# Storing the gated attention output as scaled fp16 halves and loading it through transposing DMAs

## The chip, the cores and the metric

One Trainium2 chip, one of its cores. The metric is the device time of one launch in microseconds (us). A change of under 0.2% (2.9 us here) is treated as no change.

## The reference

An encoder block for 2048 tokens of width 1024. Only the last steps bear on this change:

```python
proj = rms_norm(x, norm_w) @ w_in                     # split into u_f, g_f, q, k, v, g_a
y_f = Fourier(u_f) * silu(g_f)                        # 512 wide
# q, k, v: 3 dilation configurations x 8 slots of 64; outs and lses of each
alpha = softmax(stack(lses), axis=0)
o = sum(alpha[..., None] * stack(outs), axis=0)       # (2048, 512)
y_a = o * silu(g_a)
y = x + concatenate([y_f, y_a], axis=-1) @ w_out      # mixed is 1024 wide
```

## The kernel before

Matrix products are kept near fp32 accuracy by splitting an operand into a high and a low part and adding three products (high x high, high x low, low x high). The input projection does this with fp16 parts and weights scaled by powers of two, the output projection with parts of the type fp32r.

The work is a list of items, each one accumulation on TensorE into a PSUM tile `psq` (three buffers). Twelve units of q, k and v come first (`inproj`, L307), with the attention of earlier units beside them. Four tail units U to U+3 follow: `chan` items (L569) give gate and input of the Fourier half by channel, and `tok` items (L585), called tok 0 to tok 15 below, give the attention gate g_a for 256 tokens each, tok 0 to 7 in unit U+2 and tok 8 to 15 in unit U+3. Between tok 7 and tok 8 stand the four `chan` items of unit U+3. While one unit multiplies, `w_prep` prepares the weights `wh` of the next, in eight chunks k: ScalarE (ACT) writes the high part (L284), VectorE (DVE) the low part (L286). One step of the item loop emits everything that belongs beside the item, so every engine's order is fixed by the text of the loop in `body`; nothing is reordered afterwards.

Beside the tok items, `og_all` combines the three attention outputs: SyncE (SP) loads a tile `ot` of 256 tokens from DRAM (four buffers), POOL copies its statistics out, DVE multiplies (L696) and adds (L701, L703) into a tile `yo` (eight buffers). When tok q is through on TensorE, `ga_out` makes silu of the gate: ACT reads `psq` twice (L594, L595) into a tile `ye` (two buffers), DVE finishes silu (L596) and multiplies it into `yo` (L712). `ya_st` then stores `yo` to the DRAM tensor `YA` from SP's queue, which holds the `ot` loads and the loads `dr` of the DFT matrix (L745) as well.

After the last item comes `tail_`. SP loads `Y`, the Fourier gate, 4 MB (L853), into the room that the transposed input held, and the rows `wor` of w_out behind it (L857). The DFT runs in four parts: `f_trans` (L769, evacuated by L771 on ACT and L772 on DVE into `at`) and `f_dft` (L802, L807, evacuated by L811, L818, L819 and multiplied into `Y`). `wo_prep` splits w_out beside them (L867, L868).

The last stage is 16 rows of 128 tokens. For a row, `o_in` loads the 128 tokens of `YA` and of x, `o_mix_a` transposes `YA` on TensorE (four 128x128 transposes, L894, PSUM tile `pya`) and splits it into the tile `mx` (L895 on ACT, L896 on DVE), `o_mix_y` does the split for the Fourier half (L901, L903), and `o_mm` runs 48 matmuls of 512 columns (L917), the four attention blocks of K first. `o_in(r + 2)` stands ahead of `o_mm(r)`, and `o_mix_a(r + 1)` at its head, so in row 0 its transposes stand after the first 24 matmuls and in the others before the first.

Of the kernel before, what the change touches and what calls it, by code (L numbers as in the profile page):

```python
# [11 lines left out]
F32 = mybir.dt.float32  # L12
F32R = mybir.dt.float32r
F16 = mybir.dt.float16
BF16 = mybir.dt.bfloat16
I32 = mybir.dt.int32
AF = mybir.ActivationFunctionType
OP = mybir.AluOpType
AX = mybir.AxisListType
# [3 lines left out]
S, D = 2048, 1024  # L23
# [67 lines left out]
class Kernel:  # L91
# [615 lines left out]
    def ga_out(self, u, q):  # L707
        ps = self.PS.pop((u, q))
        y = self.YO[q].rearrange("p r w -> p (r w)")
        e = self.gp.tile([128, 2, 512], F32, name="ye", tag="ye", bufs=2)  # L710
        self.silu(e[:, 0], ps, self.W[u][1], e[:, 0], e[:, 1])
        self.nc.vector.tensor_tensor(y, y, e[:, 0], OP.mult)  # L712
        self.YD.append(q)

    def ya_st(self, q):
        hf, g = divmod(q, 8)
        dst = self.YA[g * 256:g * 256 + 256, hf * 256:hf * 256 + 256].rearrange("(r p) w -> p r w", p=128)
        self.nc.sync.dma_start(dst, self.YO.pop(q))

    def fourier_consts(self):  # L720
        nc, a = self.nc, self.a
# [137 lines left out]
    def wo_prep(self, nh, wo):  # L859
        nc = self.nc  # L860
        V, A = nc.vector, nc.scalar
        for k in range(KT):
            n = nh * KT + k + 2
            if n < 2 * KT:
                self.wo_load(*divmod(n, KT))
            raw = self.WR.pop((nh, k))
            A.copy(wo[k][:, 0], raw)  # L867
            V.tensor_tensor(wo[k][:, 1], raw, wo[k][:, 0].bitcast(F32), OP.subtract)  # L868
            yield

    def o_in0(self):
        ya = self.dp.tile([128, 2, 512], F32, name="ya0", tag="dr", bufs=2)[:, 0]
        self.nc.sync.dma_start(ya, self.YA[0:128])
        m = self.ap.tile([128, 2, 4, 512], F32R, name="mx0", tag="at", bufs=2)
        self.OI[0], self.MX[0] = ya, m[:, 0].rearrange("p a n -> p (a n)").rearrange("p (a k n) -> p a k n", a=2, k=KT)

    def o_in(self, r):
        nc = self.nc
        if r:
            self.OI[r] = ya = self.yp.tile([128, 512], F32, name="ya", tag="ya", bufs=3)  # L880
            nc.sync.dma_start(ya, self.YA[r * 128:r * 128 + 128])
        xt = self.yp.tile([128, D], F32, name="xo", tag="xo", bufs=3)
        nc.sync.dma_start(xt, self.a["x"][0, r * 128:r * 128 + 128])
        self.XO[r] = xt

    def o_mix_a(self, r):
        nc = self.nc
        V, A = nc.vector, nc.scalar
        if r:
            self.MX[r] = self.yp.tile([128, 2, KT, 128], F32R, name="mx", tag="mx", bufs=2)  # L890
        ya, m = self.OI.pop(r), self.MX[r]
        ps = (self.pso, self.psp)[r % 2].tile([128, 4, 128], F32, name="pya", tag="op"[r % 2])
        for k in range(4):
            nc.tensor.transpose(ps[:, k], ya[:, k * 128:k * 128 + 128], self.idf)  # L894
        A.copy(m[:, 0, 4:8], ps)  # L895
        V.tensor_tensor(m[:, 1, 4:8], ps, m[:, 0, 4:8].bitcast(F32), OP.subtract)  # L896

    def o_mix_y(self, r):
        m = self.MX[r]
# [28 lines left out]
    def body(self):  # L928
        tc, nc = self.tc, self.nc
        U = self.U = len(self.units)  # L930
        tail = self.tail
        with ExitStack() as ctx:
            def pool(name, bufs=1, side="left", **k):
                return tc.alloc_tile_pool(name=name, bufs=bufs, side=side, reuse_waits="tile", **k)
            psum = [pool(n, b, space=PSUM) for n, b in (("psq", 3), ("pss", 2), ("psm", 1), ("psp", 1), ("pso", 1))]
            self.psq, self.pss, self.psm, self.psp, self.pso = psum
            drm = pool("drm", space=DRAM)
# [4 lines left out]
            ctx.enter_context(tc.manual_schedule())  # L942
            self.O = [drm.tile([S, 3, 2, UW], F32, name=f"O{i}") for i in range(2)]
            self.SG = drm.tile([4, 128, S], F32, name="SG")
            self.YA = drm.tile([S, 512], F32, name="YA")
            self.KD = drm.tile([24, HD + 3], F32, name="KD")
            for d in "W WL WS PS RAW QS QR HL TR ST QW VT BT SB PB PH OB OT DT AT OI MX OW XS XR XH XP YO WR XO".split():
                setattr(self, d, {})
            self.WQ, self.OS = [], []
            self.xT = xp.tile([128, 2, KT, S], F16, name="xT")  # L950
# [47 lines left out]
            if tail:  # L998
# [8 lines left out]
                for q in range(NT):  # L1007
                    u = U + 2 + q // 8
# [20 lines left out]
            for i in range(max(len(items) + 1, G + 32)):  # L1029
                ip, wchunks = iter(()), 0  # L1030
                if i < len(items):
                    u, _, _, gen, out = items[i]
                    ip = gen()
                    p = i - first[u]
# [150 lines left out]
                    for _ in fc:  # L1185
                        pass
            if tail:
                for q in sorted(self.YO):
                    self.ya_st(q)
                self.tail_(pool, xp, fpool)  # L1190
            else:
                for c, sp in self.units:
                    nc.sync.dma_start(self.a[f"O{c}{sp}"], self.O[sp // 2][:, c, sp % 2, :])
                for p in reversed(apools):
                    p.release()
                for p in (self.wp, self.wraw, xp):
                    p.release()
# [67 lines left out]
```

## Time and profile before

| what | value |
|---|---|
| median of 3 runs | 1427.89 us (1427.65 to 1429.28) |
| the profiled execution | 1427.95 us, span 1426.2 us |
| TensorE (PE) busy | 1390.3 us, 97% of the span |
| VectorE (DVE) busy | 986.7 us, 69% |
| ScalarE (ACT) busy | 739.4 us, 52% |
| output projection, L917 | 768 matmuls, 181.3 us busy |
| transposes of YA, L894 | 64, 9.6 us busy |
| mean granted TensorE clock | 0.994 |

The profiled execution lies 0.06 us over the median, so its rows can be used as they stand. 1.75 us of it lie outside the span. Times in the rows are counted from the start of the span. A row of the timeline gives the start, the duration, the engine, the line and, in brackets, how long the engine had been idle before and what released it; a row of the chain of waits gives the start, the duration and the line that the end of the program hung on at that time.

### The profile page before, as it was taken

The numbers are of one execution on the slowest core, as the hardware profiler recorded it, in microseconds if no ns is written. First come the engines' busy times: TensorE is split into PE (matmuls) and PEld (weight loads), VectorE is DVE, ScalarE is ACT, GpSimd is POOL, SyncE is SP. The second block draws the span as 40 slices with busy tenths as digits, with TensorE's granted clock in tenths as the row PEclk, the third lists the DMA queues.
The fourth block names the chain that finished last, engine by engine and source line by source line (L and its number), as shares of the span: only waits on it lengthen the run. The fifth ranks groups of instructions, "written<-read, shape, count | busy, mean of one in ns | idle before, by whom it ended". The sixth has DMA issues, their size and how long they took to land.

```text
span 1426.2 us, 27743 instructions
## 1 busy us (share of the span) xinstructions
PE 1390.3 (97%) x9554; PEld 1027.6 (72%) x9554; DVE 986.7 (69%) x3130; ACT 739.4 (52%) x2079; POOL 458.6 (32%) x637
## 2 busy tenths in 40 slices
PE   4999999999999999999999999999999998999998
PEld 2666666667777777778888888744448697788887
DVE  6798888887878888888877777744488776611111
ACT  6676767676766666666756666554213134300110
POOL 0254444444444444444443333320000002211110
PEclk9999999999999999999999999999999999999999
DMA  7777777676766768687846465654434237333332
GB/s 212 201 142 128 143 127 142 130 140 133 136 140 121 150 117 158 119 158 115 150 101 136 99 135 97 137 110 129 147 120 136 89 102 264 103 112 111 111 117 76
DMA packets 409485, 188.66 MB, mean 132 GB/s; under 512 B 304832, under 2 KB 391040, under 8 KB 408832
## 3 DMA queue, kind: packets, MB, share of 16 engines
q1 hardware_dynamic: 380740, 173.89, 54.5%
q10 hardware_dynamic: 28604, 13.00, 3.9%
q8 instruction: 75, 1.23, 0.4%
q14 instruction: 66, 0.54, 0.1%
HBM read 72.37 MB, written 29.76 MB: 72 GB/s over the span
## 4 chain that ended last, share of the span: by engine, by line
PE 83%; DVE 6%; DMA 5%; ACT 2%; issue 2%; POOL 1%; SPq 1%; ACTq 0%; POOLq 0%; DVEq 0%
PE psq L307 44%; PE py L917 12%; PE psq L569 12%; PE psq L585 6%; PE pS L456 3%; PE po L522 2%; DMA wor<-in_w_out_dram 2%; PE po L523 1%; DMA xs<-in_x_dram 1%; PE pS L444 1%; DVE xhl L218 1%; DMA pt<-ph 1%; DMA qw<-qw 1%; DVE wh L286 1%; ACT xjk L187 0%
## 5 line engine op out<-in xcount | busy, mean ns | idle before, releaser
L307 PE MATMUL psq<-wh,xT 128*128 128x384 f16 x4608 | 789.5, 327 | 8.2 <-ACT wh L284 4.2
L307 PEld LDWEIGHTS <-xT 128*128 128x128 f16 x4608 | 541.0, 119 | 200.1 <-issue 7.1
L492 ACT ACTIVATE P<-pS,ob,kb 128x256 f32<-128x256 f32 (+1 forms) x384 | 199.4, 526 | 150.2 <-DVE ob L484 149.8
L504 POOL TENSOR_TENSOR ph<-P,ph 128x512 f16<-128x512 f32 x160 | 189.1, 1182 | 193.8 <-ACT ph L499 171.5
L360 POOL TENSOR_TENSOR qn<-qn,kb 128x128 f32<-128x128 f32 x192 | 87.5, 456 | 295.5 <-DVE qn L359 195.9
L917 PE MATMUL py<-wo,mx 128*128 128x512 f32 x768 | 181.3, 395 | 0.4 <-DVE mx L896 0.4
L569 PE MATMUL psq<-xT,wh 128*128 128x512 f16 x768 | 168.9, 379 | 0.0
L474 DVE CUSTOM_DVE_ANT_0 pS<-pS,bt 128x256 f32<-128x256 f32 (+1 forms) x384 | 147.8, 385 | 28.2 <-PE pS L444 19.8
L917 PEld LDWEIGHTS py<-wo,mx 128*128 128x128 f32 x768 | 143.2, 188 | 32.3 <-DVE mx L896 0.8
L371 POOL TENSOR_TENSOR hl<-qn,hl 128x256 f16<-128x256 f32 x192 | 130.7, 681 | 30.2 <-ACT hl L366 30.2
L569 PEld LDWEIGHTS <-wh 128*128 128x128 f16 x768 | 74.2, 98 | 87.0 <-issue 0.8
L920 DVE TENSOR_TENSOR xo<-xo,py 128x512 f32<-128x512 f32 x32 | 22.0, 688 | 139.1 <-PE py L917 139.1
L533 DVE TENSOR_REDUCE ob<-po 128x128 f32<-128x256 f32 (+1 forms) x160 | 75.3, 470 | 55.4 <-PE po L523 55.4
L499 ACT CAST ph<-P 128x512 f16<-128x512 f32 x160 | 99.0, 619 | 8.7 <-DMA wr<-in_w_in_dram 1.3
L366 ACT CAST hl<-qn 128x256 f16<-128x256 f32 x192 | 77.1, 402 | 47.6 <-POOL qn L360 37.0
L327 DVE TENSOR_TENSOR vt<-psq,vt 128x128 f16<-128x128 f32 x192 | 55.0, 286 | 62.2 <-ACT vt L326 62.0
L326 ACT CAST vt<-psq 128x128 f16<-128x128 f32 x192 | 51.2, 267 | 82.5 <-PE po L523 82.5
L286 DVE SCALAR_TENSOR_TENSOR wh<-wr,nws,wh 128x384 f16<-128x384 f32 x128 | 86.6, 682 | 2.6 <-ACT wh L284 2.6
L895 ACT CAST mx<-pya 128x512 fp32r<-128x512 f32 x16 | 9.4, 587 | 148.0 <-issue 124.9
L585 PE MATMUL psq<-wh,xT 128*128 128x256 f16 x768 | 84.3, 273 | 0.0
L585 PEld LDWEIGHTS <-xT 128*128 128x128 f16 x768 | 75.2, 98 | 9.1
L318 ACT COPY raw<-psq 128x256 f32<-128x256 f32 x192 | 69.3, 361 | 21.1 <-PE psq L307 20.6
(158 smaller groups left out, 1774.9 us busy)
## 6 DMA issues: line engine op xcount, KB each, us to landing
wr<-in_w_in_dram SPq DMA_DIRECT2D x104, 192.0 KB, 2.8
ot<-O SPq DMA_DIRECT2D x16, 792.0 KB, 4.6
st<-st SPq DMA_DIRECT2D x96, 128.0 KB, 2.6
xs<-in_x_dram SPq DMA_DIRECT2D x16, 512.0 KB, 5.3
xo<-in_x_dram SPq DMA_DIRECT2D x16, 512.0 KB, 3.5
out_dram<-xo SPq DMA_DIRECT2D x15, 512.0 KB, 2.9
O<-ob ACTq DMA_DIRECT2D x108, 66.0 KB, 2.6
O<-ob ACTq DMA_DIRECT2D x32, 132.0 KB, 2.4
```

Of the source, the lines that this page charges most:

```text
L286: V.scalar_tensor_tensor(wh[:, 1, k - 1, :n], wr[k - 1], nws[:, k - 1:k], wh[:, 0, k - 1, :n], op0=OP.mult, op1=OP.subtract)
L307: nc.tensor.matmul(ps[:, :384], self.xtile(j, k, c, t), wh[:, l, k, :384], start=n == 0, stop=n == 23)
L360: G.tensor_tensor(qn[:, 2:4], qn[:, 2:4], self.kf[:, h0:h0 + 2], OP.mult)
L366: self.nc.scalar.copy(hl.rearrange("p a h l d -> p (a h) l d")[:, :, 0], qn)
L371: self.nc.gpsimd.tensor_tensor(hv[:, :, 1], qn, hv[:, :, 0], OP.subtract)
L474: V.tensor_tensor_reduce(out=sS[:, h, cs], in0=ps[:, h, cs], in1=bs, scale=1.0, scalar=-3.0e38, op0=OP.add, op1=OP.max, accum_out=mx[:, e, ...
L492: self.nc.scalar.activation(P[:, h, cs], sS[:, h, cs], AF.Exp, bias=ob[:, e, 130 + h:131 + h], scale=self.om[:, h0 + h:h0 + h + 1], accum_ ...
L499: self.nc.scalar.copy(ph[:, 0], P)
L504: self.nc.gpsimd.tensor_tensor(ph[:, 1], P, ph[:, 0], OP.subtract)
L569: nc.tensor.matmul(ps, wh[:, l, k, col * 128:col * 128 + 128], self.xT[:, j, k, ch * 512:ch * 512 + 512], start=n == 0, stop=n == 23)
L585: nc.tensor.matmul(ps[:, j * 256:j * 256 + 256], self.xT[:, i, k, r * 128:r * 128 + 128], wh[:, l, k, 128:384], start=n % 24 == 0, stop=n ...
L917: nc.tensor.matmul(ps[nh], m[:, j, k], wo[nh][k][:, l], start=(j, l, k) == (0, 0, 4), stop=(j, k) == (1, 3))
```

## The change

`ga_out` scales y by a power of two and splits it into two fp16 halves: ACT writes the high half (new L718), DVE the low half (new L719), both into the second half of the tile `ye`. The scale comes from a bound on y over the column half, computed by four small DVE instructions ahead of tok 0 and tok 8 (`ya_scale`, new L727 to L730). `ya_st` stores the two halves from `ye` with two DMAs (new L737), so a buffer of `ye` is free only when both have landed. `o_in` loads each half with a transposing DMA (new L899, L908), and `o_mix_a` only converts to fp32r: one copy on ACT (new L919), one on DVE (new L920). The inverse of the scale goes into the rows of w_out that belong to the attention half (new L891, L892 beside L887, L888).

```diff
     def ga_out(self, u, q):
...
-        self.nc.vector.tensor_tensor(y, y, e[:, 0], OP.mult)
+        V = self.nc.vector
+        V.tensor_tensor(y, y, e[:, 0], OP.mult)
+        if q % 8 == 0:
+            self.ya_scale(q // 8, self.W[u][1])
+        sc = self.YS[q // 8][:, 0:1]
+        h = e[:, 1].bitcast(F16).rearrange("p (l n) -> p l n", l=2)
+        self.nc.scalar.activation(h[:, 0], y, AF.Copy, scale=sc)
+        V.scalar_tensor_tensor(h[:, 1], y, sc, h[:, 0], op0=OP.mult, op1=OP.subtract)
+        self.YO.pop(q)
+        self.YH[q] = h
         self.YD.append(q)
+
+    def ya_scale(self, hf, sb):
+        V = self.nc.vector
+        t = self.YS[hf] = self.sm.tile([128, 2], F32, name="ysc", bufs=2)
+        V.tensor_reduce(t[:, 1:2], self.IS[:, hf].rearrange("p c s h -> p (c s h)"), AX.X, OP.max)
+        V.scalar_tensor_tensor(t[:, 1:2], t[:, 1:2], 2.0 ** 16, sb[:, 1:2], op0=OP.mult, op1=OP.mult)
+        V.tensor_scalar(t[:, 0:1].bitcast(I32), t[:, 1:2].bitcast(I32), 0x7F800000, None, op0=OP.bitwise_xor)
+        V.tensor_scalar(t[:, 1:2], t[:, 1:2], 0.5, None, op0=OP.mult)
 
     def ya_st(self, q):
         hf, g = divmod(q, 8)
-        dst = self.YA[g * 256:g * 256 + 256, hf * 256:hf * 256 + 256].rearrange("(r p) w -> p r w", p=128)
-        self.nc.sync.dma_start(dst, self.YO.pop(q))
+        h = self.YH.pop(q)
+        for l in range(2):
+            dst = self.YA[l, g * 256:g * 256 + 256, hf * 256:hf * 256 + 256].rearrange("(r p) w -> p r w", p=128)
+            self.nc.sync.dma_start(dst, h[:, l].rearrange("p (r w) -> p r w", r=2))
...
     wo_prep:
-            A.copy(wo[k][:, 0], raw)
-            V.tensor_tensor(wo[k][:, 1], raw, wo[k][:, 0].bitcast(F32), OP.subtract)
+            if k < 4:
...
+            else:
+                sc = self.YS[k // 2 - 2][:, 1:2]
+                A.activation(wo[k][:, 0], raw, AF.Copy, scale=sc)
+                V.scalar_tensor_tensor(wo[k][:, 1], raw, sc, wo[k][:, 0].bitcast(F32), op0=OP.mult, op1=OP.subtract)
...
     o_in (o_in0 alike, into ya0):
-            self.OI[r] = ya = self.yp.tile([128, 512], F32, name="ya", tag="ya", bufs=3)
-            nc.sync.dma_start(ya, self.YA[r * 128:r * 128 + 128])
+            self.OI[r] = ya = self.yp.tile([128, 2, 4, 128], F16, name="ya", tag="ya", bufs=3)
+            for l in range(2):
+                nc.sync.dma_start(ya[:, l], self.YA[l, r * 128:r * 128 + 128], transpose=True)
...
     o_mix_a:
-        ps = (self.pso, self.psp)[r % 2].tile([128, 4, 128], F32, name="pya", tag="op"[r % 2])
-        for k in range(4):
-            nc.tensor.transpose(ps[:, k], ya[:, k * 128:k * 128 + 128], self.idf)
-        A.copy(m[:, 0, 4:8], ps)
-        V.tensor_tensor(m[:, 1, 4:8], ps, m[:, 0, 4:8].bitcast(F32), OP.subtract)
+        A.copy(m[:, 0, 4:8], ya[:, 0])
+        V.tensor_copy(m[:, 1, 4:8], ya[:, 1])
```

The order of the instructions on VectorE, from tok 5 to the last weight chunk of unit U+3 (the last L286). Before:

```order
L596 SCALAR_TENSOR_TENSOR ye<-ye 128x512
L712 TENSOR_TENSOR yo<-yo,ye 128x512
L670 TENSOR_TENSOR cr<-cs 128x16
L672 TENSOR_TENSOR cw<-cw,IS 128x48
L674 TENSOR_TENSOR cr<-cr,cs 128x16
L286 SCALAR_TENSOR_TENSOR wh<-wr,nws,wh 128x384
L676 RECIPROCAL cr<-cr 128x16
L678 TENSOR_TENSOR cw<-cw,cr 128x48
L596 SCALAR_TENSOR_TENSOR ye<-ye 128x512
L712 TENSOR_TENSOR yo<-yo,ye 128x512
```

After, at the same place:

```order
L596 SCALAR_TENSOR_TENSOR ye<-ye 128x512
L713 TENSOR_TENSOR yo<-yo,ye 128x512
L719 SCALAR_TENSOR_TENSOR ye<-yo,ysc,ye 128x512
L670 TENSOR_TENSOR cr<-cs 128x16
L672 TENSOR_TENSOR cw<-cw,IS 128x48
L674 TENSOR_TENSOR cr<-cr,cs 128x16
L286 SCALAR_TENSOR_TENSOR wh<-wr,nws,wh 128x384
L676 RECIPROCAL cr<-cr 128x16
L678 TENSOR_TENSOR cw<-cw,cr 128x48
L596 SCALAR_TENSOR_TENSOR ye<-ye 128x512
```

L719 stands right behind the product that it reads (L713), with nothing between them while ACT computes L718, and ahead of the weight chunks.

SP's queue in the same stage (loads `ot`, stores `YA`), as one piece of the difference:

```order
-L718 DMA YA<-yo 128x2x256 x3
+L737 DMA YA<-ye 128x2x256 x6
 L645 DMA ot<-O_102 128x2x792 x2
-L718 DMA YA<-yo 128x2x256 x4
+L737 DMA YA<-ye 128x2x256 x8
 L645 DMA ot<-O_102 128x2x792 x2
-L718 DMA YA<-yo 128x2x256
+L737 DMA YA<-ye 128x2x256 x2
```

The stores keep their places: those of tok 3 stand behind two `ot` loads, as before, but now a buffer of `ye` hangs on them.

More of the change, by code (lines that the diff above doesn't have):

```diff
@@ L866, in wo_prep @@
             raw = self.WR.pop((nh, k))
-            A.copy(wo[k][:, 0], raw)
-            V.tensor_tensor(wo[k][:, 1], raw, wo[k][:, 0].bitcast(F32), OP.subtract)
+            if k < 4:
+                A.copy(wo[k][:, 0], raw)
+                V.tensor_tensor(wo[k][:, 1], raw, wo[k][:, 0].bitcast(F32), OP.subtract)
+            else:
+                sc = self.YS[k // 2 - 2][:, 1:2]
+                A.activation(wo[k][:, 0], raw, AF.Copy, scale=sc)
+                V.scalar_tensor_tensor(wo[k][:, 1], raw, sc, wo[k][:, 0].bitcast(F32), op0=OP.mult, op1=OP.subtract)
             yield
@@ L872, in o_in0 @@
         ya = self.dp.tile([128, 2, 512], F32, name="ya0", tag="dr", bufs=2)[:, 0]
-        self.nc.sync.dma_start(ya, self.YA[0:128])
+        ya = ya.bitcast(F16).rearrange("p (l k n) -> p l k n", l=2, k=4)
+        for l in range(2):
+            self.nc.sync.dma_start(ya[:, l], self.YA[l, 0:128], transpose=True)
         m = self.ap.tile([128, 2, 4, 512], F32R, name="mx0", tag="at", bufs=2)
@@ L879, in o_in @@
         if r:
-            self.OI[r] = ya = self.yp.tile([128, 512], F32, name="ya", tag="ya", bufs=3)
-            nc.sync.dma_start(ya, self.YA[r * 128:r * 128 + 128])
+            self.OI[r] = ya = self.yp.tile([128, 2, 4, 128], F16, name="ya", tag="ya", bufs=3)
+            for l in range(2):
+                nc.sync.dma_start(ya[:, l], self.YA[l, r * 128:r * 128 + 128], transpose=True)
         xt = self.yp.tile([128, D], F32, name="xo", tag="xo", bufs=3)
@@ L944, in body @@
             self.SG = drm.tile([4, 128, S], F32, name="SG")
-            self.YA = drm.tile([S, 512], F32, name="YA")
+            self.YA = drm.tile([2, S, 512], F16, name="YA")
             self.KD = drm.tile([24, HD + 3], F32, name="KD")
-            for d in "W WL WS PS RAW QS QR HL TR ST QW VT BT SB PB PH OB OT DT AT OI MX OW XS XR XH XP YO WR XO".split():
+            for d in "YH YS W WL WS PS RAW QS QR HL TR ST QW VT BT SB PB PH OB OT DT AT OI MX OW XS XR XH XP YO WR XO".split():
                 setattr(self, d, {})
@@ L1187, in body @@
             if tail:
-                for q in sorted(self.YO):
+                for q in sorted(self.YH):
                     self.ya_st(q)
```

## The prediction

> **What bounds the kernel now.** I read the windows by stage first, then the chain of waits, then the timeline where the change touches VectorE (DVE) and ScalarE (ACT).
>
> ```profile
> core 0: us, PE busy (x) PEld busy (x) DVE busy (x) ACT busy (x) POOL busy (x), PEclk, DMA share, GB/s
> 1060.00:1120.00 60.00, 60.00 (x471) 45.85 (x470) 51.72 (x112) 16.83 (x31) 5.01 (x14) 1.00 0.40 131
> 1251.00:1423.00 172.00, 171.53 (x771) 139.91 (x770) 30.11 (x45) 15.25 (x28) 18.00 (x14) 1.00 0.31 107
> ```
>
> TensorE (PE) is busy in both stages that change. In the output rows (the second window) DVE is nearly idle. In the first window, where tok 0 to 7 run, DVE is busy for 51.72 of 60 us: an engine off the path, with little left.
>
> The chain of waits shows what the transposes cost:
>
> ```profile
> 1244.11 0.66 PE pya L894 x4
> ...
> 1250.31 0.44 PE pya L894 x4
> 1250.75 11.06 PE py L917 x48
> ...
> 1399.95 0.44 PE pya L894 x4
> ```
>
> Each output row is 11.06 to 11.08 us of matmuls and a group of four transposes. There are 15 such groups on the chain: 0.66 us for row 1 and 14 of 0.44 (the first and the last stand above).
>
> **What the change removes.** 14 x 0.44 + 0.66 = 6.82 us, and the 0.30 us that PE idles ahead of row 1's group for its DMA (first row below; the number in brackets is the idle time). Row 0's own transposes give nothing: PE waits behind them for DVE's split anyway (second row), and DVE's order there stays.
>
> ```profile
> 1244.11 0.66 PE L894 MATMUL pya<-idf,ya 128*128 128x128 f32 x4 [0.30 <-DMA ya<-YA]
> 1238.44 5.37 PE L917 MATMUL py<-wo,mx 128*128 128x512 f32 x22 [0.36 <-DVE mx L896]
> 1241.55 0.33 SPq L881 DMA_DIRECT2D ya<-YA  x1
> ```
>
> There, DVE's copy of the low half may be shorter than the subtraction it replaces, by at most its 0.69 us, once. I take 7.1 us, between 6.5 and 7.5. The new L891 and L892 have the operands of L867 and L868 and a scale more; I cost them at nothing to 0.3 us.
>
> **What it adds: a hand-off from DVE to ACT and back for every tok.** DVE makes y (L713), ACT the high half (L718), DVE the low half (L719), which is next in DVE's order, so DVE stands still meanwhile. None of the two has run here in its shape; their neighbours have:
>
> ```profile
> L284 ACT ACTIVATE wh<-wr,nws x128: 600/612/625, 18.2 to 1101.1; 128x384 f16<-128x384 f32 x128
> L210 ACT ACTIVATE xhl<-xs,xri 128x1024 f16<-128x1024 f32 x16 | 18.4, 1153 | 9.8 <-DVE xri L112 9.8
> L286 DVE SCALAR_TENSOR_TENSOR wh<-wr,nws,wh x128: 525/614/1092, 18.9 to 1109.9; 128x384 f16<-128x384 f32 x128
> L218 DVE SCALAR_TENSOR_TENSOR xhl<-xs,xri,xhl x16: 1266/1284/1699, 12.3 to 90.1; 128x1024 f16<-128x1024 f32 x16
> 1157.60 0.68 ACT L595 ACTIVATE ye<-psq,scb 128x512 f32<-128x512 f32 x1
> 1158.31 0.69 DVE L596 SCALAR_TENSOR_TENSOR ye<-ye 128x512 f32<-128x512 f32 x1 [2.82 <-ACT ye L595]
> L661 DVE TENSOR_TENSOR cm<-cn 128x16 f32<-128x16 f32 x6 | 1.0, 167 | 0.0
> ```
>
> At 512 columns, on the line between 384 and 1024, L718 takes 0.72 us and L719 0.75. A hand-over costs 0.03 (1158.28 to 1158.31). So DVE loses 0.72 + 0.75 + 2 x 0.03 = 1.53 us per tok, and 4 x 0.17 = 0.7 more for the scale at tok 0 and tok 8.
>
> **First place: the weights of unit U+3.** DVE's seven hand-offs of tok 0 to 6 stand ahead of the last weight chunk.
>
> ```profile
> 1102.91 0.60 DVE L286 SCALAR_TENSOR_TENSOR wh<-wr,nws,wh 128x384 f16<-128x384 f32 x1
> 1109.84 20.88 PE L569 MATMUL psq<-xT,wh 128*128 128x512 f16 x96
> 1109.88 0.61 DVE L286 SCALAR_TENSOR_TENSOR wh<-wr,nws,wh 128x384 f16<-128x384 f32 x1
> DVE ye L596 <- ACT ye L595: 4.6, 3, 2.2
>   ACT ye L595: 12.9, 8
> ```
>
> The first two rows of DVE are chunks 6 and 7, the last two of eight. The unit begins at 1109.84; a matmul takes 20.88 / 96 = 0.2175 us, and the low part of chunk 7 is first read by the 23rd, at 1109.84 + 22 x 0.2175 = 1114.6. The chunk is ready at 1110.49: the cover is 4.1 us. The hand-offs add 7 x 1.53 + 0.7 = 11.4. DVE idles ahead of L596 for 4.6 us from 1060 to 1131 (fourth row: three waits, the longest 2.2) and for 12.9 us in all (fifth), and the lag may use these gaps up; that leaves at least 11.4 - 4.6 = 6.8, a chunk at 1117.3 and a stall of 2.7 us. That is the floor.
>
> I take more, because `ye` now waits for its stores. The stores of tok 3 stand in SP's queue behind two loads of `ot`, and the second of these waits for DVE's L703:
>
> ```profile
> 1096.81 0.68 DVE L703 TENSOR_TENSOR yo<-yo,ot 128x512 f32<-128x512 f32 x1
> 1099.96 0.67 ACT L594 ACTIVATE ye<-psq,scb 128x512 f32<-128x512 f32 x1
> 1101.24 0.69 DVE L596 SCALAR_TENSOR_TENSOR ye<-ye 128x512 f32<-128x512 f32 x1 [0.88 <-ACT ye L595]
> ot<-O SPq DMA_DIRECT2D x1, 792.0 KB, 4.6
> YA<-yo SPq DMA_DIRECT2D x1, 256.0 KB, 4.8
> ```
>
> L703 ended at 1097.49; four hand-offs and the scale (6.8) make it 1104.3. Two issues of 0.4 later the second store goes out at 1105.1, and a store just behind an `ot` took 4.8 us to land (last row, issued at 1115.90): 1109.9. Only then may L594 of tok 5 write its buffer, 10.0 us later than now, with L596 at 1111.2. Tok 5 and 6 add 3.1, the gap ahead of tok 6 takes back its 2.2: chunk 7 is 10.9 us late, at 1121.4, a stall of **6.8 us**. With nothing taken back it is 9.0. Behind the waiting L594 on ACT stand the high part of chunk 7 and the readings of `psq`; behind the waiting L719 on DVE stand the chunks. Both are in this lag. SP issues 16 more stores at 0.4 us, which matter only where a row hangs on them.
>
> Chunk 6 comes at 1103.51 + 10.0 + 1.53 = 1115.0, for 1109.84 + 19 x 0.2175 = 1114.0; after it PE has three matmuls, then stands still from 1115.7 to 1121.4, 5.7 us on end. What such a pause does to PE's clock (the third number from the end of a window row) is seen elsewhere in this trace:
>
> ```profile
> 1210.94 2.04 PE L769 MATMUL ptr<-BD,F 128*128 128x128 f32 x8 [6.95 <-DVE pe L819]
> 1204.00:1208.00 4.00, 0.00 (x0) 0.00 (x0) 3.97 (x4) 1.31 (x3) 2.24 (x2) 0.82 0.41 131
> 1208.00:1212.00 4.00, 1.05 (x5) 1.09 (x6) 3.93 (x6) 0.00 (x0) 4.00 (x4) 0.50 0.79 262
> 1216.00:1220.00 4.00, 4.00 (x17) 3.18 (x17) 0.77 (x1) 2.34 (x3) 0.00 (x0) 0.90 0.00 0
> ```
>
> PE idled from 1203.99; a mean clock of 0.82 in 4 us is 1.4 us at half speed, so it fell 2.6 us into the pause. It stayed at 0.50 until 0.8 us into the last window: 5.9 us of work at half speed, **2.9 us** lost. I add that; a stall of under 2.6 us would not bring it. The Trainium skill (TensorE: Matmul & The Clock Gate, Part 1) puts the time to come back at about 3.4 us of sustained work, which would cost 1.7 us and the sum 1.2 us less; the row above is longer, and decides.
>
> **Second place: tok 8 to 15 and the start of the DFT.**
>
> ```profile
> 1131.48 1.22 DVE L622 TENSOR_TENSOR eT<-uT 128x1023 f32<-128x1023 f32 x1 [8.30 <-ACT uT L616]
> 1174.75 0.69 DVE L712 TENSOR_TENSOR yo<-yo,ye 128x512 f32<-128x512 f32 x1
> 1175.92 2.01 SPq L853 DMA_DIRECT2D Y<-SG  x4
> 1177.98 12.55 DMA wor<-in_w_out_dram
> 1190.56 0.63 ACT wo L867
> ```
>
> At 1131.48 DVE had idled 8.30 us, so the old lag is paid back, and DVE starts again with PE's shift. To the L712 of tok 15 it gets 7 x 1.53 + 0.7 = 11.4 us more; the gaps ahead of L596 here are 12.9 - 4.6 = 8.3. If all are used, 3.1 stays; if none, 11.4. I take 6.7 of the 8.3, an estimate: gaps behind ACT's L666, itself waiting for DVE, move with the lag. That leaves **4.7 us**. Then tok 15 needs its own L718 and L719 and one more issue before SP comes to the load of `Y`: 1.53 + 0.4 = **1.9 us**. The chain goes on through that load to `wor` and ACT's L867, so all of it moves the DFT and the output rows.
>
> **Sum.** 6.8 + 2.9 + 4.7 + 1.9 - 7.1 = +9.2 us, on the profiled execution's 1427.95, which is 0.06 above the median: **1437 us**.
>
> The transposing loads themselves I cost at nothing, hidden under 11.1 us of matmuls per row:
>
> ```profile
> xo<-in_x_dram SPq DMA_DIRECT2D x16, 512.0 KB, 3.5
> out_dram<-xo SPq DMA_DIRECT2D x15, 512.0 KB, 2.9
> st<-hl SPq DMA_TRANSPOSE x192, 2.8
> pt<-ph SPq DMA_TRANSPOSE x160, 3.5
> ```
>
> `st` is one of 128x512, the shape of a half; both start a row ahead. Row 1's are issued at 1241.55 and needed at 1249.4 (1250.31 less the 0.66 and 0.30 that go), 7.8 us later; without cover each late us would count once.
>
> **Rivals.**
> A, only the floor: the stores of tok 3 land in time and the clock stays. 2.7 + 0 + 3.1 + 1.9 - 7.1 = +0.6, up to +4 with part of the waits: 1428.5 to 1432. For it: a half is 128 KB where the row has 256. Against it: the store's place behind `ot`.
> B, faster: the hand-off is short enough to live in DVE's gaps. It decides at 7 h + 0.7 - 4.6 = 4.1, a hand-off h of 1.14 us: then PE never waits for the weights, the second place costs 7 x 1.14 + 0.7 - 8.3 = 0.4, the end 1.14 + 0.4, and 1.9 - 7.1 = -5.2 gives 1422.8. Against it are the rows of L284 and L286, which take 1.23 together at 384 columns alone.
> C, the output rows become bound by SP's queue: if its four transfers ran one after the other, 2 x 3.5 + 3.5 + 2.9 = 13.4 us against 11.08, 2.3 x 14 = 32 us, 1469. Against it: the DMA engines are busy for 0.31 of this stage. The Trainium skill (VectorE: DVE Perf Modes, The three transpose paths) gives 1309 ns for a 128x128 block by DMA and 390 ns on TensorE, and advises TensorE where PSUM will do; by it eight blocks a row would be 10.5 us, the row 16.9 and the whole some 1518, an estimate that shares C's chance. The trace disagrees: `pt` moves eight such blocks and lands in 3.5 us.
>
> **How the numbers follow.** Forecast, 1432 to 1444: 0.74. A: 0.13, half of it within 0.2% (2.9 us, about what a measurement can tell from no change). B: 0.07. C: 0.03, other slower ways 0.03. The top takes the stall of 9.0, a second drop of the clock while PE waits for the first DFT part, 6 us at the second place and the smallest gain: 9.0 + 2 x 2.9 + 6 + 1.9 - 6.5 = 16.2, 1444. The range is 1428 to 1444, which leaves out B, C and the rest. Faster 0.07, same 0.07, slower 0.86.
>
> **What would show it.** Right: PE idle inside L569 at the start of unit U+3, released by DVE L286, with a clock near 0.5 behind it; DVE idle ahead of L719, 16 times some 0.8 us; ACT L594 of tok 5 released by a DMA; the load of `Y` some 16 us later; rows of 11.08 us with no gap. Wrong: no wait of PE for `wh`, an L594 that never waits for a store, or output rows over 11.1 us.

## The result, and the profile after

| kernel | median | runs | ratio to before, 95% interval |
|---|---|---|---|
| before | 1427.81 us | 4 (1427.65 to 1429.28) | |
| changed | 1441.18 us | 4 (1438.13 to 1443.20) | 1.0087 (1.0074 to 1.0099) |

The change costs 13.4 us. The profiled execution of the changed kernel took 1441.58 us, its span is 1439.7 us, its mean clock 0.990. Line numbers of the changed kernel are used from here: the product is L713, the halves are L718 (ACT) and L719 (DVE), the load of `Y` is L872, the output projection L941.

Start where PE waits. These are all waits of PE from 1060 to 1250 us (total, times, longest):

```profile
PE ptr L788 <- DVE pe L838: 5.9, 1, 5.9
PE ptr L788 <- DVE at L791: 4.7, 1, 4.7
PE psq L569 <- ACT ye L595: 3.4, 1, 3.4
PE psq L569 <- DVE wh L286: 2.3, 1, 2.3
```

The first was there before (6.95 us, quoted in the prediction). The other three are new: one in the DFT, two at the start of unit U+3. The wait for `wh` was forecast; the one for ACT's L595 was not: it is for a buffer of `psq`, not for weights. The chain of waits shows why L595 was late:

```profile
1107.82 0.42 SPq L737
1108.24 0.05 issue
1108.29 6.45 DMA YA<-ye
1114.85 0.69 ACT ye L594
1115.53 0.59 ACT ye L595
...
1116.87 0.70 DVE yo L713
...
1118.41 0.75 DVE ye L719
```

The first row issues the high half of tok 3. The second store, the low half, is issued at 1108.29 and lands after 6.45 us, and only then may L594 of tok 5 write its buffer of `ye`. L595 reads the `psq` tile of tok 5 for the last time, so PE gets that buffer only at 1116.16. On the timeline of PE, and of DVE for the last weight chunk:

```profile
1116.16 7.85 PE L569 MATMUL psq<-xT,wh 128*128 128x512 f16 x22 [3.42 <-ACT ye L595]
1125.63 0.61 DVE L286 SCALAR_TENSOR_TENSOR wh<-wr,nws,wh 128x384 f16<-128x384 f32 x1
1126.30 4.06 PE L569 MATMUL psq<-xT,wh 128*128 128x512 f16 x18 [2.29 <-DVE wh L286]
```

The 22 matmuls between the two waits take 7.85 us where 22 x 0.2175 would be 4.8. The windows say why (third number from the end is PE's clock):

```profile
1112.00:1116.00 4.00, 0.74 (x7) 0.51 (x6) 0.00 (x0) 1.15 (x2) 0.35 (x2) 0.91 0.31 91
1116.00:1120.00 4.00, 3.84 (x10) 1.32 (x10) 2.97 (x8) 2.46 (x5) 0.00 (x0) 0.50 0.12 35
1120.00:1124.00 4.00, 4.00 (x14) 1.41 (x12) 3.08 (x6) 1.91 (x4) 0.00 (x0) 0.73 0.22 66
```

The clock falls at about 1115.3 (a mean of 0.91 is 0.09 x 4 / 0.5 = 0.7 us at half speed, ahead of 1116) and is back at about 1122.2. Some 6 us of work run at half speed, 3.0 us lost. 3.4 + 2.3 + 3.0 = 8.7 us for the first place, close to the +9.0 counted from a marker below.

The hand-off itself, from the view of the tile `ye` (duration: min/median/max; then idle time ahead of the readers and writers of `ye`):

```profile
L718 ACT ACTIVATE ye<-yo,ysc x16: 721/722/722, 1083.8 to 1192.0; 128x512 f16<-128x512 f32 x16
L719 DVE SCALAR_TENSOR_TENSOR ye<-yo,ysc,ye x16: 750/752/753, 1084.5 to 1192.7; 128x512 f16<-128x512 f32 x16
  ACT ye L718: 13.2, 16
  DMA YA<-ye: 3.4, 1
```

16 waits of 0.83 us on DVE ahead of L719, and 0.75 for L719 itself. The second place and the output rows, from the timeline and the chain:

```profile
1193.97 2.01 SPq L872 DMA_DIRECT2D Y<-SG  x4
1256.00 1.58 DVE L920 CAST mx<-ya 128x512 fp32r<-128x512 f16 x1
1257.64 178.49 PE py L941 x766
1436.15 0.69 DVE xo L944
L908 SPq DMA_TRANSPOSE ya<-YA x30: 1195/1276/2696, 1260.7 to 1405.5; - x30
```

The load of `Y` goes out 18.05 us later than before. From 1257.64 to 1436.15 the chain holds nothing but matmuls: all 16 rows run without a gap, so the transposing loads are hidden. (L908's numbers are the time to issue one; none is on the chain.) But row 0 begins with a new wait: its copy L920 takes 1.58 us, against 0.42 in the other rows, while POOL runs L841.

**Where the 13 us went.** Not all of it is the change's. The marker L265, two matmuls at the end of the attention, stood at 1071.62 us before and at 1074.37 here, though nothing ahead of it differs. The kernel before, profiled a second time (below), had it at 1073.29. So I count every later event from that marker; the two profiles of before then agree within 0.1 us up to the load of `Y`, and within 1.0 at the end (351.0 and 349.9, mean 350.4).

| from the marker, us | last L286 starts | L622 of ct 3 | product of tok 15 | load of Y | last xo |
|---|---|---|---|---|---|
| before | 38.3 | 59.9 | 103.1 | 104.3 | 350.4 |
| changed | 51.3 | 68.8 | 116.8 | 119.6 | 361.8 |
| later by | 13.0 | 9.0 | 13.7 | 15.3 | 11.3 |

Read as steps (from the unrounded times): first place +9.0, second place +4.7, end +1.6, output rows (with the DFT ahead of them) -4.0; sum +11.3. The remaining 2 us of the 13.4 lie within the spread of the part ahead of the marker.

### The profile page after: what moved, and what is told of

It is laid out like the page before. It is cut to its first block, busy times and chain, and to the rows that moved or that the text cites. A ratio compares the mean times of both kernels' runs of the same rounds, so it can differ in the third digit from the quotient of the medians.

```text
span 1439.7 us, 27737 instructions
## 1 busy us (share of the span) xinstructions
PE 1389.9 (97%) x9490; PEld 1024.8 (71%) x9490; DVE 995.4 (69%) x3154; ACT 751.7 (52%) x2095; POOL 459.5 (32%) x637
## 4 chain that ended last, share of the span: by engine, by line
PE 75%; DVE 12%; DMA 5%; ACT 4%; issue 3%; POOL 1%; SPq 1%; ACTq 0%; POOLq 0%; DVEq 0%
PE psq L307 43%; PE py L941 12%; PE psq L569 11%; PE pS L456 3%; PE po L522 2%; DMA wor<-in_w_out_dram 1%; PE po L523 1%; DVE ot L696 1%; PE pS L444 1%; DVE xhl L218 1%; DMA qw<-qw 1%; DMA xs<-in_x_dram 1%; DVE wh L286 1%; DMA pt<-ph 1%; DVE yo L713 1%
## 5 line engine op out<-in xcount | busy, mean ns | idle before, releaser
L941 PE MATMUL py<-wo,mx 128*128 128x512 f32 x768 | 179.1, 395 | 1.9 <-DVE mx L920 1.9
L569 PE MATMUL psq<-xT,wh 128*128 128x512 f16 x768 | 172.0, 384 | 5.7 <-ACT ye L595 3.4
L941 PEld LDWEIGHTS py<-wo,mx 128*128 128x128 f32 x768 | 145.3, 189 | 35.5 <-DVE mx L920 2.3
L326 ACT CAST vt<-psq 128x128 f16<-128x128 f32 x192 | 51.3, 267 | 85.3 <-PE po L523 85.3
L286 DVE SCALAR_TENSOR_TENSOR wh<-wr,nws,wh 128x384 f16<-128x384 f32 x128 | 86.2, 679 | 2.6 <-ACT wh L284 2.6
L919 ACT CAST mx<-ya 128x512 fp32r<-128x512 f16 x16 | 9.9, 622 | 138.2 <-PE py L941 130.9
L318 ACT COPY raw<-psq 128x256 f32<-128x256 f32 x192 | 69.6, 362 | 20.8 <-PE psq L307 20.1
```

Source lines behind the costliest of these rows:

```text
L286: V.scalar_tensor_tensor(wh[:, 1, k - 1, :n], wr[k - 1], nws[:, k - 1:k], wh[:, 0, k - 1, :n], op0=OP.mult, op1=OP.subtract)
L569: nc.tensor.matmul(ps, wh[:, l, k, col * 128:col * 128 + 128], self.xT[:, j, k, ch * 512:ch * 512 + 512], start=n == 0, stop=n == 23)
L941: nc.tensor.matmul(ps[nh], m[:, j, k], wo[nh][k][:, l], start=(j, l, k) == (0, 0, 4), stop=(j, k) == (1, 3))
```

## The experiments

Theory: the hand-off loses DVE about 1.6 us per tok; together with `ye` waiting for its stores it makes the weights of unit U+3, the DFT and `Y` late, and the tail gives back part of it. Main rival: the stores and transposing DMAs are to blame. Each ratio is to runs of the kernel before on the same chip, so two variants are best compared by their ratios.

### The tail alone

```diff
-        V.tensor_tensor(y, y, e[:, 0], OP.mult)
-        ... (scale, L718, L719)
+        h = y.bitcast(F16).rearrange("p (l n) -> p l n", l=2)
+        V.tensor_tensor(h[:, 0], y, e[:, 0], OP.mult)   # both stores of ya_st send h[:, 0]
```

The inverse scale in w_out (L891, L892) is left out too. The stores leave from `yo`, so this kernel says nothing of `ye` waiting for them.

> The split into halves is left out (no L718, no L719, no scale): the product is written once as fp16 and stored into both planes of YA, so the output is not the reference's; the two stores per tok, the transposing loads and the new mix of the output rows are those of the changed kernel. Theory (the hand-off of the halves, and ye waiting for its stores, lose the time; the transposing loads cost nothing; the transposes give back what was measured in the profile after, 5.6 us from the first py to the end): L622 and L713 of tok 15 stand where they stood before (1131.5 and 1174.8 us, give or take the 3 us by which the attention differs from run to run), the Y load at most 0.6 us later, and the time is 1421 to 1423 us, 5 to 7 us under before. Rival 1 (the two stores and the transposing loads themselves lose the time, on SP's queue or in the DMA engines): 1428 us or more. Rival 2 (the transposes were hidden and give nothing, the 5.6 us are row 0's alone): 1427 to 1428 us.

Measured: 1423.11 us (1421.45 to 1424.11, 5 runs) against 1428.66; ratio 0.9958 (0.9945 to 0.9970), 5.5 us faster. Last L286, L622 and product of tok 15 stand at 38.3, 59.9 and 103.1 us from the marker, as before, and the load of `Y` at 104.8. PE's waits from 1060 to 1260:

```profile
PE ptr L783 <- DVE pe L833: 7.2, 1, 7.2
PE py L936 <- DVE mx L915: 1.7, 1, 1.7
```

Neither `wh` nor `psq` is waited for. Twice the stores and 32 transposing loads cost nothing that shows, and taking the transposes off TensorE is worth 5.5 us. Both rivals fall.

### The hand-off alone

```diff
-            self.YA = drm.tile([2, S, 512], F16, name="YA")
+            self.YA = drm.tile([S, 512], F32, name="YA")     # the halves side by side
... (o_in0, o_in and o_mix_a of the kernel before)
```

> The hand-off and the stores of the changed kernel, word for word, but the halves lie side by side in an fp32 YA and are loaded and transposed by TensorE as the kernel before does it: the values are not the reference's. Theory: the changed kernel without its gain from the first py on, 1441.2 + 5.7 to 7.1 = 1447 to 1448 us; the sum of this run's and of the tail-alone run's differences from before is the changed kernel's +13.4 within 1 us. Rival (the transposing loads delay something between the hand-off and the output rows, or PE's clock): this run stays below 1445 us, and the differences don't add up.

Measured: 1448.79 us (1446.05 to 1449.28, 4 runs), ratio 1.0136 (1.0122 to 1.0150), +20.1 us. PE waits where it did in the changed kernel:

```profile
PE psq L569 <- DVE wh L286: 5.2, 1, 5.2
PE ptr L788 <- DVE at L791: 4.7, 1, 4.7
PE psq L569 <- ACT ye L595: 3.1, 1, 3.1
```

The two halves of the change add up: +20.1 - 5.5 = +14.6 against +13.4 measured together, 1.2 us apart where 1 was expected, and inside the spread of the runs. The whole loss lies with the hand-off and its stores from `ye`, none of it with the transposing loads.

### The halves in yo instead of ye

```diff
+        p = e[:, 0]
+        V.tensor_tensor(p, y, p, OP.mult)
-        h = e[:, 1].bitcast(F16)...
+        h = y.bitcast(F16)...              # yo has 8 buffers, ye has 2
```

> The same work on every engine as in the changed kernel; only the buffers change places: the product goes to ye, the halves to yo, so that ye (2 buffers) comes free with L719 and never waits for a store, while yo (8 buffers) waits for it as before. Theory (the store in front of ye made the psq wait of 3.4 us and, with DVE's hand-off, the wh wait and the clock's fall): no wait of PE for L595 at the start of the unit, a wait for wh of at most 2.7 us (the prediction's floor) at a clock that does not fall there, L622 of ct 3 at +2.7 instead of +9.0 us, the second place unchanged at +4.7: 1434 to 1436 us. Rival (DVE's and ACT's hand-off alone makes the stall, the store was no part of it): 1440 to 1442 us, as the changed kernel.

Measured: 1438.40 us (1436.25 to 1439.77, 5 runs), ratio 1.0065 (1.0051 to 1.0079): 2.8 us better than the changed kernel (3.1 by the ratios, whose intervals just overlap), where 5 to 7 were expected. Neither the theory's 1434 to 1436 us nor the rival's 1440 to 1442 came true.

```profile
PE ptr L789 <- DVE pe L839: 6.4, 1, 6.4
PE psq L569 <- DVE wh L286: 4.9, 1, 4.9
PE ptr L789 <- DVE at L792: 4.2, 1, 4.2
1116.00:1120.00 4.00, 0.64 (x3) 0.10 (x1) 3.18 (x4) 1.87 (x3) 0.00 (x0) 0.84 0.23 66
1120.00:1124.00 4.00, 2.49 (x6) 0.87 (x7) 3.96 (x6) 0.00 (x0) 0.00 (x0) 0.50 0.18 29
1124.00:1128.00 4.00, 4.00 (x16) 1.66 (x15) 3.14 (x6) 1.30 (x2) 0.83 (x2) 0.81 0.44 173
```

The wait for `psq` is gone, so the stores did make that one. The wait for `wh` is larger, not smaller: 4.9 us, and the clock falls (windows, last three rows). So DVE's hand-off alone makes a stall of 4.9 us, not the 2.7 that the prediction took as its floor, and the 4.0 us of work at half speed behind it (1121.5 to 1125.5) add 2.0: L622 of ct 3 is 7.0 us late, where 2.7 were expected. The last L286 stands 9.1 us later than before: 7 x 1.53 + 0.7 = 11.4 less 2.3, where the prediction had let the lag use up 4.6 us of DVE's gaps. The gaps ahead of L596 still sum to 2.3 us here (1.46 at tok 1, 0.87 at tok 5); only the gap at tok 6 is used up.

### The low half on POOL

```diff
-        V.scalar_tensor_tensor(h[:, 1], y, sc, h[:, 0], op0=OP.mult, op1=OP.subtract)
+        self.nc.gpsimd.tensor_tensor(h[:, 1], p, h[:, 0], OP.subtract)   # the scale is in z (L595)
```

> The whole computation, with the hand-off taken off DVE: the scale goes into z (L595), the product goes to ye already scaled, ACT writes the high half into yo and POOL subtracts for the low half. DVE has per tok what it had before; ACT has 0.72 us more, POOL about 1.2 us more (its L504, the same shape, as the nearest row). Theory (DVE's standing still for ACT and its second pass are what delays wh, the transposes of the DFT and the Y load): first place 0 to 1 us, second place 0 to 1 us, the end +2.6 us (0.75 on ACT, 1.2 on POOL, the second issue ahead of the Y load), output rows -5.7: 1422 to 1427 us, most likely 1425. Rival (POOL beside DVE slows DVE, as L920 took 1.58 us for 0.42 beside POOL's L841, or POOL's copies that wait for ot loads hold ye): 1430 us or more.

Measured: 1432.08 us (1429.88 to 1434.98, 8 runs), ratio 1.0025 (1.0014 to 1.0035). This was a miss: 0.25% slower than before where a gain was expected. The profile shows the fastest of the eight executions (1429.88 us). PE's wait and, grouped from 1060 to 1260 us, DVE's and POOL's rows (sum, mean ns):

```profile
PE psq L569 <- DVE wh L286: 3.0, 1, 3.0
L701 DVE TENSOR_TENSOR yo<-ot 128x512 f32<-128x512 f32 x13 | 13.2, 1013 | 0.3
L286 DVE SCALAR_TENSOR_TENSOR wh<-wr,nws,wh 128x384 f16<-128x384 f32 x8 | 6.1, 784 | 0.8 <-ACT wh L284 0.8
L719 POOL TENSOR_TENSOR yo<-ye,yo 128x512 f16<-128x512 f32 x16 | 26.2, 1640 | 97.2 <-ACT yo L718 97.2
1116.00:1120.00 4.00, 1.04 (x6) 0.32 (x5) 3.97 (x5) 1.49 (x3) 1.95 (x1) 1.00 0.22 66
```

DVE has fewer instructions than in the changed kernel, yet two of them take longer: L701 has a mean of 1013 ns (690 with the halves in `yo`), L286 784 (610 before). The expectation had this as its rival, and the rival holds. The means hide how it happens; the timeline shows it:

```profile
1101.61 1.75 DVE L696 TENSOR_TENSOR ot<-ot,cw 128x1536 f32<-128x1536 f32 x1
1102.42 1.96 POOL L719 TENSOR_TENSOR yo<-ye,yo 128x512 f16<-128x512 f32 x1 [4.34 <-ACT yo L718]
1103.40 1.53 DVE L701 TENSOR_TENSOR yo<-ot 128x512 f32<-128x512 f32 x1
```

The two take turns. POOL's L719 takes 1.15 to 1.16 us in seven of its sixteen executions. In seven others it starts while DVE's L696 runs, takes 1.95 to 2.56 us and ends 1.00 to 1.03 us after L696. L701 takes 0.68 to 0.72 us in eight of thirteen; the five that start while L719 runs take 1.52 to 1.53 and end 0.53 to 0.55 us after L719. L696, which starts first, takes its 1.75 us throughout. The Trainium skill (Trainium Architecture — The Big Picture, What this means for kernel authors) says that DVE and GpSimd (POOL) share a port pair under an exclusive lock. These rows agree: the second of the two is held until the first is through. Which pairs of instructions are held this way, no run here tells. The stall was 3.0 us here, and the clock stayed at 1.00 (last row).

### The hand-off postponed

Buffers as in the kernel with the halves in `yo`, but ACT's high half is emitted at the end of the item, behind the weight chunks, and DVE's low half in the next item, behind two steps of the attention's sum. DVE then no longer stands still for the high half (except behind tok 15, the last).

```diff
+                self.ga_lo()                 # DVE, ahead of the stores of the next item
                 while self.YD:
                     self.ya_st(self.YD.pop(0))
...
+                self.ga_hi()                 # ACT, behind the chunks of wh
                 ao, ao2, ao3 = b0, ao, ao2
```

> The halves in yo as in the run before, and both of their instructions later in the order: ACT writes the high half of a tok at the end of its item, behind the chunks of wh; DVE the low half in the next item, behind two steps of the attention's sum. Neither engine stands still for the other; DVE's own 0.75 us per tok stays. Theory (what costs is DVE's time per tok, 1.6 us with the wait for ACT; the profile before leaves room for about 1.1, which was the condition of the prediction's rival B): no wait of PE for wh or psq, full clock, L713's place of tok 15 within 1 us of before, the end +2, the output rows -5.6: 1423 to 1427 us, most likely 1424.5. Rival (DVE has no room at all, each 0.75 us goes on the path): the last wh 4.5 us later than before at tok 5, some 3 us of waits in the first place and 6 in the second: 1431 us or more.

Measured: 1423.35 us (1422.43 to 1427.21, 5 runs) against 1429.24, ratio 0.9968 (0.9956 to 0.9981): faster than both kernels, and the whole computation. PE's waits, and the time of the low half:

```profile
PE ptr L798 <- DVE pe L848: 8.0, 1, 8.0
PE py L951 <- DVE mx L930: 1.9, 1, 1.9
PE ptr L798 <- DVE at L801: 0.4, 1, 0.4
L729 DVE SCALAR_TENSOR_TENSOR yo<-ye,ysc,yo x16: 659/745/752, 1083.2 to 1177.0; 128x512 f16<-128x512 f32 x16
```

DVE still spends 0.75 us per tok, but the last L286 is only 1.2 us later than before, the product of tok 15 only 0.5, the load of `Y` 2.0. The profiled execution (1425.26 us) is one of the slower of the five.

### The same with the low half computed twice

```diff
             self.nc.vector.scalar_tensor_tensor(h[:, 1], p, sc, h[:, 0], op0=OP.mult, op1=OP.subtract)
+            self.nc.vector.scalar_tensor_tensor(h[:, 1], p, sc, h[:, 0], op0=OP.mult, op1=OP.subtract)
```

> As the postponed hand-off, but DVE writes the low half twice: DVE has 1.5 us more per tok than in the kernel before, all of it work, with no standing still and no store in front of ye. Theory (DVE's time per tok decides, whether it works or waits; room about 1.1 us): PE waits for wh again (2 to 5 us), and the second place grows by 2 to 5 us: 1430 to 1438 us. Rival (the order of the hand-off, its wait for ACT, ACT's L284 behind it, is what costs, not DVE's load): within 2 us of the postponed kernel.

Measured: 1429.34 us (1427.82 to 1432.00, 11 runs), ratio 1.0004 (0.9995 to 1.0012).

```profile
PE ptr L799 <- DVE at L802: 4.0, 1, 4.0
PE psq L569 <- DVE wh L286: 0.4, 1, 0.4
```

Neither side was quite right. The second pass costs 6.0 us, so DVE's load counts. Counted from the marker, L622 of ct 3 is 0.5 us later than before, the product of tok 15 3.8, the load of `Y` 6.1: the second place grew by 3.2 us, within the 2 to 5 expected. But PE waits only 0.4 us for `wh`, less than the 2 to 5 expected, and the kernel is 9 us faster than the one with the halves in `yo`, whose DVE loses nearly the same 1.5 us per tok. Its last L286 is 4.6 us late instead of 9.1. Part of this is position: the last L286 stands behind tok 6's own hand-off in the one order (1.5 us) and ahead of it in the other. Most of the rest grows at tok 1 and tok 5 (1.3 and 1.1 us between the products of the two kernels), and the rows of L596 show why: there DVE with the halves in `yo` still waits for ACT (1.46 and 0.87 us, the gaps that its hand-offs did not use up), while here it does not wait, since the low half stands between L596 and the work before it.

### Postponed, with the halves in ye again

```diff
-        p = e[:, 0]
+        p = y                                # and h in e[:, 1], as in the changed kernel
```

> The postponed hand-off with the buffers of the changed kernel: the product stays in yo, the halves go to ye, so that ye waits for its stores again; only the order of the instructions differs from the changed kernel. Theory (the store in front of ye is a cost of its own, decided by the store of tok 3, which goes out beside two ot loads and then lands after 6.5 us instead of 2): L594 of tok 5 some 3 us later than in the postponed kernel, the last wh 3 us later, at 1114 to 1116 us, PE's wait for it 0 to 3 us without a fall of the clock: 1424 to 1429 us. Rival (with the order mended the store is covered): within 1 us of the postponed kernel's 1423.4 us. If the store costs here what it cost beside the unmended order (the changed kernel against the halves in yo, 2.8 us): 1426 us.

Measured: 1426.44 us (1422.55 to 1428.74, 12 runs), ratio 0.9982 (0.9973 to 0.9991), 3.1 us over the postponed kernel (2.0 by the ratios) with overlapping intervals. ACT's waits for the stores from 1076 to 1190, and the one of the two in the first place:

```profile
ACT ye L594 <- DMA YA<-ye: 4.0, 2, 2.4
1106.68 0.69 ACT L594 ACTIVATE ye<-psq,scb 128x512 f32<-128x512 f32 x1 [2.37 <-DMA YA<-ye]
```

The store holds L594 for 2.4 us and the last L286 is 3.7 us late instead of 1.2, as expected, but PE does not wait for it in the profiled execution. (The store landed 4.4 us after its issue, not the 6.5 expected.) The other wait, 1.6 us, is at 1148.78. Counted from the marker, the last xo stands at 347.9 us here and in the postponed kernel, so the two profiles show no cost of the store at all; where the 3.1 us of the medians come from stays open.

### Postponed, with row 0's copy on ACT

```diff
-        V.tensor_copy(m[:, 1, 4:8], ya[:, 1])
+        (V.tensor_copy if r else A.copy)(m[:, 1, 4:8], ya[:, 1])
```

> As the postponed hand-off, and for row 0 alone the copy of the low half (L920 of the changed kernel, 1.58 us on DVE beside POOL's L841, for 0.42 elsewhere) goes to ACT. Theory (PE's 1.9 us wait ahead of the first py is that copy): 0.6 to 1.3 us under the postponed kernel, the wait for mx at most 1.2 us. Rival (the first py waits for the DFT's last instructions anyway): within 0.3 us of it.

Measured: 1422.63 us (1421.64 to 1425.51, 5 runs), ratio 0.9956 (0.9942 to 0.9969), the best of all. Of PE's three waits in the postponed kernel two are left:

```profile
PE ptr L798 <- DVE pe L848: 8.3, 1, 8.3
PE ptr L798 <- DVE at L801: 0.5, 1, 0.5
```

The wait for `mx` is gone. The last xo stands 344.5 us from the marker instead of 347.9: the wait of 1.9 us is gone, and so is a fall of the clock behind it (3.4 us at half speed, 1.7 us). But the medians differ by 0.7 us only, with overlapping intervals: the cause of that wait is shown, its worth is not.

### The kernel before once more

Unchanged, for the marker alone.

> The kernel before, unchanged, profiled a second time. The marker L265 of the last unit stood at 1071.6 us in its first profile and at 1073.4 to 1075.0 in those of the changed kernel and four variants, whose program is the same up to there. If that differs from execution to execution, this profile can stand anywhere from 1071 to 1075; if every variant really loses 2 us before the attention's end, it stands at 1071.6 within 0.5.

Measured: 1428.60 us, one run. The marker in the first and the second profile of the same kernel:

```profile
1071.62 0.39 PE L265 MATMUL pm<-idf,am 128*128 128x128 f32 x2
1073.29 0.39 PE L265 MATMUL pm<-idf,am 128*128 128x128 f32 x2
```

Over all eleven profiles it lies between 1071.62 and 1075.60, in the postponed kernel at 1071.95. It differs from execution to execution of one and the same kernel, so the changed kernel's +2.75 cannot be put down to the change.

## Why the prediction was right, and where its steps were off

The time came out at 1441.18 us, 4 over the forecast of 1437 and inside 1428 to 1444. Step by step:

| step | predicted | measured |
|---|---|---|
| hand-off per tok | 1.53 us | 0.75 + 0.83 of standing still = 1.58 |
| first place, with the clock | 6.8 + 2.9 = +9.7 | +9.0 |
| second place | +4.7 | +4.7 |
| end | +1.9 | +1.6 |
| transposes and output rows | -7.1 | -4.0 |

The 4 us between forecast and result are 3.1 us of the last step, some 2 us ahead of the marker that are not the change's, less 1.0 us by which the first and third steps were taken too high. That the sum came so near is partly luck, as the first and the last point show.

- **The stall at the weights** was right in its sum and wrong in its make-up. The second store of tok 3 was issued at 1108.29, which less 2.75 for the marker is 1105.5 (the prediction had 1105.1, and left out the 0.4 us of an `ot` issue), but landed after 6.45 us, not 4.8. The last chunk came 13.0 us late, not 10.9. PE stalled for it only 2.3 us because it already stood 3.4 us for `psq`, which the prediction did not see: L595 of tok 5, held by the same store, also frees the tile in which the unit's first item accumulates. And the fall of the clock was not added, as the prediction had it: the work at half speed (until 1122.2) ran while PE would have waited for `wh` anyway (until 1126.3), so the lag of the chunk alone sets the loss. The two errors, a chunk 2.1 us later and a clock counted beside the wait, nearly cancelled.
- **The cover of 4.1 us** (chunk ready at 1110.49, needed at 1114.6) was the best term. The lag of the last L286 less 4.13 (the cover unrounded) gives 4.9, 3.0 and 0.4 us for the kernels with lags of 9.06 (halves in yo), 7.16 (POOL) and 4.56 (twice); PE waited 4.9, 3.0 and 0.4. At lags of 1.2 and 3.7 (postponed) it did not wait at all. For the changed kernel it gives 13.0 - 4.1 = 8.9, its whole loss at this place.
- **The floor of 2.7 us** and with it rival A were wrong. Without any store in the way the stall is 4.9 us, since the lag uses up 2.3 us of DVE's gaps and not 4.6: the waits of L596 for ACT at tok 1 and tok 5 move along with it. A would not have been 1428.5 to 1432 but the 1438.4 of the kernel with the halves in `yo`.
- **Rival B** named the right quantity: a hand-off short enough for DVE's gaps would be faster, 1422.8 us. With 0.75 us per tok, and DVE not standing, the time is 1423.35. The condition (1.14 us) was of the right size: at 1.5 us the time is that of the kernel before. The nearness of 1423.35 to 1422.8 is partly luck: in the profiled execution the last xo stands only 2.5 us earlier than before, counted from the marker.
- **The second place** rested on an estimate that 6.7 of the 8.3 us of gaps ahead of L596 would be used. It held: behind 1131 the changed kernel has 1.9 us of them left, so 6.4 to 6.5 were used. The second drop of the clock, which only the top of the range held, came too (PE waited 4.7 us for `at`, and the clock stood at 0.50 from about 1193.8 to 1200.4). It cost nothing that shows: from the load of `Y` to the first `py` the changed kernel takes 61.2 us, the two profiles of before 61.5 and 60.2.
- **The price of a fall of the clock** was read from one row. The 5.9 us of work at half speed in it are 3.3 in the second profile of the same kernel, behind a pause of nearly the same length (6.8 us), which would make 1.7 us of the 2.9. And "a stall of under 2.6 us would not bring it" is refuted by row 0, next.
- **The tail's gain** was mis-sized by 3 us, at row 0. The step that failed is row 0's copy: the prediction let it be shorter than the subtraction that it replaces, by up to 0.69 us. Beside POOL's L841 it took 1.58 us (the subtraction had taken 0.68), PE waited 1.9 us for it instead of 0.4, and the clock fell again. The two windows of 8 us from 1252 on, and under them the window with the same wait in the kernel with the tail alone:

```profile
1252.00:1260.00 8.00, 6.14 (x25) 4.61 (x24) 7.40 (x11) 0.46 (x1) 4.50 (x3) 0.92 0.01 3
1260.00:1268.00 8.00, 8.00 (x32) 6.43 (x31) 2.75 (x4) 1.30 (x3) 0.72 (x1) 0.87 0.59 131
```

```profile
1236.00:1244.00 8.00, 6.30 (x28) 4.81 (x27) 7.21 (x11) 0.62 (x1) 5.15 (x3) 1.00 0.00 0
```

0.08 x 8 + 0.13 x 8 = 1.7 us, and 7.1 - 1.5 - 1.7 = 3.9, against 4.0 measured. With the tail alone the wait was there, the fall was not, and 5.5 us came back. In all seven kernels in which DVE makes this copy it takes 1.58 us and ends 0.28 us after POOL's instruction beside it; the subtraction of the kernel before (L896, 1237.70 to 1238.38) ran beside the same instruction of POOL (L822, 1237.26 to 1239.00) and was not held up. One of its operands lies in PSUM, the copy's lies in SBUF; whether that makes the difference, no run tells.
- **Rival C** is refuted for these loads: PE waits for none of them in 16 rows, in the changed kernel or in any variant that has them.

## What to carry to other kernels

An instruction that asks another engine for its operand costs its own engine the other's time too (here 0.83 us beside 0.75 of its own); where that engine is as busy as DVE was here (86%), put the request at one place in the order and the use a step later, and let work stand between them. That order was worth more here (1438.40 to 1423.35 us) than the buffers (1441.18 to 1438.40). Where a result changes its tile, ask what else waits for the tile: a store in front of a scratch buffer held up a PSUM buffer two items later. And a deadline with its cover (ready at, needed at) is worth working out exactly: with the lags read from their traces it gave PE's waits in variants built later to 0.1 us.

## What the runs showed of the hardware that I had not expected

- The length of a pause alone does not tell whether PE's clock falls. Ahead of row 0 it fell in five kernels behind pauses of 1.86 to 2.14 us (the changed kernel's windows above), 2.5 to 2.9 us after the pause began, when PE was already at work again. It stayed at 1.00 behind pauses of 1.70 us (tail alone) and 2.06 us (POOL) at the same place. At the weights a pause of 3.0 us (POOL) left it at 1.00, one of 4.9 us (halves in yo) brought it to 0.50. The Trainium skill (TensorE: Matmul & The Clock Gate, Part 1) tells of a free-running window of about 3.4 us; a window with a phase of its own could give both answers at 3.0 us, but a fall after a pause of 1.9 us does not fit a whole idle window.
- The work needed to bring the clock back differed too, in one and the same kernel: 5.9 us and 3.3 us in the two profiles of before. It was 4.0 us, from 1121.5 (PE's first matmul) to about 1125.5, with the halves in `yo`, and some 6.0 us, from 1116.2 to 1122.2, in the changed kernel.
- DVE and POOL held each other up: a single copy took 3.7 times as long (L920, 0.42 to 1.58 us), L701 1.5 times on average over a stage (690 to 1013 ns). In the rows of the kernel with the low half on POOL the one that starts second ends a fixed time after the first. L896 beside POOL's L822 was not held up.
